# Gate and up projections as seven block products for eight, and a down projection over eight PSUM banks

## Chip, cores and metric

The kernel runs on one core of one Trainium2 chip. The metric is the device time of one launch in microseconds (us). All inputs start in HBM and the result ends there.

## What is computed

Two transformer blocks run one after the other on 512 tokens of width 1024, in float32. Each ends in a gated feed-forward network (FFN); the change touches these two FFNs and what stands next to them. Cut to that:

```python
# block 1, after attention
h = rms_norm(x, norm_ffn_pre)
f = (silu(h @ w_gate) * (h @ w_up)) @ w_down      # 1024 -> 2816 -> 1024
x = x + rms_norm(f, norm_ffn_post)
# block 2: mixer (pooling, stick-breaking attention, gates), then
h = rms_norm_2(x, norm_ffn)
x = x + (silu(h @ w_ffn_gate) * (h @ w_ffn_up)) @ w_ffn_down
gate = sigmoid(rms_norm_2(x, norm_ple) @ w_ple_gate)
x = x + gate * (p @ w_ple_proj)
return rms_norm_2(x, norm_final)
```

## The kernel before

**Precision.** A float32 matrix product is made from three products of a reduced format: each operand is split into a high part (a ScalarE copy) and a low part (a subtraction), and `mm3` (L138 to L140) adds hi·hi, hi·lo and lo·hi in one PSUM bank. So every weight tile of 128x1024 is loaded by a DMA on SP's queue (L131), its high part is made on ACT (L132) and its low part (L133) on DVE, or on POOL where `pl["lo"]` says so. Activations are split in the same way by `split_from` (L225, L226) and `split_many` (L213, L218).

**The FFN.** The 2816 hidden features are 22 f tiles of 128. For one f tile, `glu` multiplies the gate's and the up's weight tile (8 blocks of 128 input features each) with all 512 tokens: 2 x 8 x 3 = 48 matmuls of 128x512. Then come silu on ACT (L660), the product with up on DVE (L661, one operand in PSUM), and the split of the result, whose low part (L226) is POOL's. `ffn` takes the f tiles in three groups (6, 8, 8); after each group it loads that group's rows of the down weights and makes the down product, token tile by token tile (128 tokens, two banks of 512), and `evac` adds the banks to an SBUF accumulator (L707, L709, L1011).

**Where an FFN begins.** The first `NFIRST = 4` f tiles run on tokens 0 to 255 first and on tokens 256 to 511 afterwards, in matmuls of 256 columns, since the norms of token tiles 2 and 3 come late (`late_norm`, `norm_fill`; `tr_fill` transposes a normed tile with TensorE, L175, and splits it). The low parts of these tiles' weights are POOL's.

**Where an FFN ends.** The first FFN's last `evac1` calls `post_norm_then_pre` (L1073 to L1079): mean square on ACT (L166), reciprocal root on DVE (L148 to L159), scale by the gain row (L1076), add to x (L1077), norm again (`scale_rows`, L1070). x stays in SBUF, and is also written to memory (`spill` x2, L716) for block 2.

**What sets the order.** The program is written in Python loops over a tile framework, which gives each engine its own instruction order by priorities (`tc.high_priority`) and gives out buffers from pools. A new tile waits until the last reader of the buffer's old tile is done. All big loads are on SP's queue in one order, so a load that waits for its buffer holds back those behind it.

## Time and profile before

| | |
|---|---|
| time, median of 3 runs (lowest to highest) | 1372.39 us (1371.35 to 1376.75) |
| the profiled execution's own time, its span | 1375.31 us, 1373.5 us |
| TensorE clock granted, mean | 0.988 |
| busy: TensorE (PE), weight loads (PEld) | 1324.0 us (96%), 1080.8 us (79%) |
| busy: VectorE (DVE), ScalarE (ACT), GpSimd (POOL) | 715.1 (52%), 595.1 (43%), 250.2 (18%) |
| read from HBM | 130.14 MB, 101 GB/s over the span |

Times in the profile count from the span's start. The first FFN lies at about 231 to 612 us, the second at about 943 to 1308 us. Line numbers are those of the kernel before; where a line of the changed kernel is meant, the text says so.

### The profile page before, as it was taken

To read this page: it belongs to the slowest core of one execution; us is meant where nothing else is said; L and a number is where in the kernel's file an instruction comes from. 1 tells how busy PE (TensorE), PEld (TensorE's weight loads), DVE (VectorE), ACT (ScalarE), POOL (GpSimd) and SP (SyncE) were. 2 spreads that over 40 slices of the span, in tenths; PEclk is the share of its full clock that TensorE was granted. 3 is DMA by queue.
4 is the path that set the end of the run, shared out by engine and by line. 5 is a ranking of instruction groups with operands and counts; after the bars stand their busy time and mean duration, and the time that the engine had idled before them with its cause. 6 is when DMAs were issued, how large, how long until landed. Compare 5 with 4: busy or idle time off the path is not lost.

```text
span 1373.5 us, 17214 instructions
## 1 busy us (share of the span) xinstructions
PE 1324.0 (96%) x6476; PEld 1080.8 (79%) x6476; DVE 715.1 (52%) x1399; ACT 595.1 (43%) x1087; POOL 250.2 (18%) x255
## 2 busy tenths in 40 slices
PE   8889998899999999999999999989999999999997
PEld 6656666798888888878777778879988888888886
DVE  5889677742433242386886672655423321422464
ACT  5578876340322132244866564524413220422252
POOL 1433234320111011100323010115210110021002
PEclk9999999899999999999999999999999999999999
DMA  7212123241533143223121435634424330532031
GB/s 271 92 31 78 47 74 111 93 138 47 153 92 107 39 146 98 71 93 100 63 77 54 130 132 192 198 108 143 134 77 121 95 106 17 160 115 93 1 108 62
DMA packets 44771, 139.64 MB, mean 102 GB/s; under 512 B 7312, under 2 KB 7696, under 8 KB 44688
## 3 DMA queue, kind: packets, MB, share of 16 engines
q1 hardware_dynamic: 44544, 138.54, 31.8%
q8 instruction: 51, 0.84, 0.2%
q14 instruction: 32, 0.26, 0.1%
q10 hardware_dynamic: 144, 0.00, 0.0%
HBM read 130.14 MB, written 8.39 MB: 101 GB/s over the span
## 4 chain that ended last, share of the span: by engine, by line
PE 76%; DVE 9%; issue 7%; ACT 3%; POOL 2%; DMA 1%; POOLq 0%; ACTq 0%; DVEq 0%
PE acc L139 10%; PE acc L140 10%; PE acc L138 10%; PE f L140 10%; PE f L138 10%; PE f L139 10%; PE av L139 3%; PE av L138 3%; PE av L140 3%; DVE wt L133 2%; PE av L475 1%; DVE p L858 1%; PE tp L468 1%; DMA raw<-in_w_out 1%; PE tp L175 1%
## 5 line engine op out<-in xcount | busy, mean ns | idle before, releaser
L133 DVE TENSOR_TENSOR wt<-raw,wt 128x1024 fp32r<-128x1024 f32 (+1 forms) x204 | 254.2, 1247 | 280.8 <-ACT wt L132 279.8
L132 ACT ACTIVATE wt<-raw 128x1024 fp32r<-128x1024 f32 (+1 forms) x220 | 231.3, 1056 | 352.4 <-issue 84.2
L138 PE MATMUL f<-u,wt 128*128 128x512 f32 (+1 forms) x556 | 210.8, 379 | 4.3 <-DVE u L575 4.1
L139 PE MATMUL f<-u,wt 128*128 128x512 f32 (+1 forms) x556 | 210.0, 378 | 0.2 <-DVE u L218 0.2
L140 PE MATMUL f<-u,wt 128*128 128x512 f32 (+1 forms) x556 | 209.6, 377 | 0.0
L226 POOL TENSOR_TENSOR u<-t,u 128x512 fp32r<-128x512 f32 (+1 forms) x52 | 82.1, 1580 | 541.0 <-ACT u L225 541.0
L139 PE MATMUL acc<-u,wt 128*128 128x512 f32 (+1 forms) x432 | 155.0, 359 | 0.0
L138 PE MATMUL acc<-u,wt 128*128 128x512 f32 (+1 forms) x432 | 154.9, 359 | 0.0
L140 PE MATMUL acc<-u,wt 128*128 128x512 f32 (+1 forms) x432 | 154.8, 358 | 0.0
L138 PEld LDWEIGHTS f<-u,wt 128*128 128x128 f32 x556 | 106.3, 191 | 23.1 <-DVE u L575 4.3
L138 PE MATMUL f<-wt,u 128*128 128x512 f32 x302 | 120.6, 399 | 2.1 <-ACT u L225 2.1
L140 PE MATMUL f<-wt,u 128*128 128x512 f32 x302 | 119.9, 397 | 1.4 <-DVE u L226 1.4
L139 PEld LDWEIGHTS f<-u,wt 128*128 128x128 f32 x556 | 106.4, 191 | 17.1 <-DVE u L218 0.4
L140 PEld LDWEIGHTS f<-u,wt 128*128 128x128 f32 x556 | 106.4, 191 | 16.9
L139 PE MATMUL f<-wt,u 128*128 128x512 f32 x302 | 119.4, 396 | 0.0
L138 PE MATMUL acc<-wt,u 128*128 128x512 f32 (+1 forms) x288 | 112.7, 391 | 5.9 <-ACT wt L132 5.9
L139 PE MATMUL acc<-wt,u 128*128 128x512 f32 (+1 forms) x288 | 112.8, 392 | 1.6 <-DVE wt L133 1.5
L140 PE MATMUL acc<-wt,u 128*128 128x512 f32 (+1 forms) x288 | 112.4, 390 | 0.0
L138 PEld LDWEIGHTS acc<-u,wt 128*128 128x128 f32 x432 | 82.2, 190 | 12.0
L140 PEld LDWEIGHTS acc<-u,wt 128*128 128x128 f32 x432 | 82.0, 190 | 11.9
L139 PEld LDWEIGHTS acc<-u,wt 128*128 128x128 f32 x432 | 82.0, 190 | 11.8
L661 DVE TENSOR_TENSOR t<-t,acc 128x512 f32<-128x512 f32 (+1 forms) x52 | 31.4, 604 | 94.4 <-PE acc L140 91.3
(257 smaller groups left out, 2138.0 us busy)
## 6 DMA issues: line engine op xcount, KB each, us to landing
raw<-in_w_out SPq DMA_DIRECT2D x24, 512.0 KB, 3.7
raw<-in_w_gate SPq DMA_DIRECT2D x22, 512.0 KB, 3.6
raw<-in_w_up SPq DMA_DIRECT2D x22, 512.0 KB, 3.6
raw<-in_w_down SPq DMA_DIRECT2D x22, 512.0 KB, 3.6
raw<-in_w_ffn_gate SPq DMA_DIRECT2D x22, 512.0 KB, 3.5
raw<-in_w_ffn_up SPq DMA_DIRECT2D x22, 512.0 KB, 3.5
raw<-in_w_ffn_down SPq DMA_DIRECT2D x22, 512.0 KB, 3.5
raw<-in_w_in SPq DMA_DIRECT2D x11, 512.0 KB, 5.5
```

The source lines that it names most:

```text
L132: nc.scalar.activation(w[:, 0, c], raw[:, c], AF.Copy)
L133: pl["lo"].tensor_tensor(w[:, 1, c], raw[:, c], w[:, 0, c].bitcast(F32), op=ALU.subtract)
L138: nc.tensor.matmul(ps, lhsT=st[0], rhs=mv[0], start=first, stop=False)
L139: nc.tensor.matmul(ps, lhsT=st[0], rhs=mv[1], start=False, stop=False)
L140: nc.tensor.matmul(ps, lhsT=st[1], rhs=mv[0], start=False, stop=last)
L175: nc.tensor.transpose(pt[:, j * P:(j + 1) * P], h_t[:, k * P:(k + 1) * P], ident)
L226: (lo_eng or nc.vector).tensor_tensor(lo, src, hi.bitcast(F32), op=ALU.subtract)
L468: nc.tensor.transpose(pt[:, c:c + P], pn[j][:, kc * P:(kc + 1) * P], ident)
L475: nc.tensor.matmul(o[s * 64:s * 64 + 64], lhsT=VT[kc][:, kv], rhs=ts[s][:, i * 256:i * 256 + 256], start=kc == 0, stop=kc == NT - 1, skip_ ...
L661: nc.vector.tensor_tensor(s[:, :n], s[:, :n], pu[:, :n], op=ALU.mult)
L858: nc.vector.tensor_tensor_scan(c[:, n - 1::-1], ones.to_broadcast([P, n]) if nq == 1 else restart[:, :n], e[:, n - 1::-1], 0.0, op0=ALU.mu ...
```

## The change

Tokens are cut into two halves of 256 and the 1024 input features into two halves of 512; gate and up are the two block columns of one 2 by 2 block matrix. Seven products of blocks take the place of eight. Each product (`prod`, L309 of the changed kernel) has 4 feature blocks x 3 parts = 12 matmuls of 128x256, so an f tile has 84 of these.

- Left operands: a11 and a12 are transposed token rows as before (`left_raw`). a22 and four sums of blocks (p1, s2, s3, p4) come from `left_rest`: for each of two pairs of token tiles four subtractions of 128x512 on DVE, five blocks of four transposes, and their splits. An FFN has 56 transposes where it had 32.
- Right operands: `Tile.sums` forms four sums of weight halves on POOL (128x512, in place in the load buffers), one f tile ahead, and splits the two 1024-wide results; `prepare` loads both weight tiles and splits the gate's tile and half of the up's.
- `Tile.rest` combines the products: five DVE operations of 128x256 with one operand in PSUM, two silu of 128x256, one ACT copy, and one product of 128x512 on DVE. The low part of the result moves from POOL to DVE.
- The FFN begins with `NFIRST = 6` tiles, of which only the first two products run early; they need tokens 0 to 255 alone. Their gate weights' low parts are DVE's. Both late norms come before the FFN.
- f tiles come in groups (6, 5, 5, 6). `down` keeps all 4 x 2 PSUM banks open and goes through the group's f tiles with one 128x1024 row tile of the down weights at a time (528 matmuls of 128x512 for an FFN, as before), after the next group's first f tile. The last group goes token tile by token tile.
- x is written out before the first FFN and loaded again in `evac1`; the gain rows there use the load buffers (`raw_tile`, five in turn). The loads of the side input p move behind the second FFN.

```diff
-NFIRST = 4
+NFIRST = 6
...
+    GROUPS = (6, 5, 5, 6)
...
+    def raw_tile():
+        pools = pl["raws"]
+        cnt[4] += 1
+        return pools[cnt[4] % len(pools)].tile([P, 1024], F32, tag="raw", name=nm("raw"))
...
+    def left_rest(X, h0, h1, j):
+
+        c1, c2 = u_tile([P, 2, 512]), u_tile([P, 2, 512])
+        sub = nc.vector.tensor_tensor
+        sub(c1[:, 0], h1[:, 0:512], h1[:, 512:1024], op=ALU.subtract)
+        sub(c1[:, 1], h0[:, 0:512], c1[:, 0], op=ALU.subtract)
+        left_block(X, "s2", c1[:, 1], j)
...
+    def prod(ps, w, off, X, first):
+
+        for k in range(4):
+            x = X[k // 2][:, k % 2]
+            st = wcols(w, off + k * P, off + (k + 1) * P)
+            mv = (x[:, 0], x[:, 1])
+            for n, (a, b) in enumerate(((0, 0), (0, 1), (1, 0))):
+                nc.tensor.matmul(ps[:, :256], lhsT=st[a], rhs=mv[b], start=first and k == 0 and n == 0,
+                                 stop=k == 3 and n == 2, skip_group_check=True)
...
+        def prepare(self):
+
+            self.G, self.U = load_raw(self.wg[self.f]), load_raw(self.wu[self.f])
+            if not self.head:
+                self.wG = w8(self.G, pl["wt"])
+            self.w22 = w4(self.U[:, 512:1024])
+
+        def sums(self):
+
+            lo, hi = slice(0, 512), slice(512, 1024)
+            G, U = self.G, self.U
+            add = nc.gpsimd.tensor_tensor
+            add(G[:, lo], G[:, lo], U[:, lo], op=ALU.add)
+            add(U[:, lo], U[:, lo], U[:, hi], op=ALU.add)
+            add(U[:, hi], G[:, lo], U[:, hi], op=ALU.add)
+            self.wb = w8(U, wt1)
+            add(G[:, hi], U[:, hi], G[:, hi], op=ALU.add)
+            self.wa = w8(G, wt1)
...
+            if after:
+                after.first()
+            up = t_tile([P, 2, 256])
+            pn = any8()
+            prod(pn, wb, 512, X["s2"], True)
+            tt(E[:, 1], pn[:, h], E[:, 0], op=ALU.subtract)
+            pq = any8()
+            prod(pq, wb, 0, X["s3"], True)
+            tt(up[:, 1], E[:, 1], pq[:, h], op=ALU.subtract)
+            pr = any8()
+            prod(pr, wa, 0, X["p1"], True)
+            tt(up[:, 1], pr[:, h], up[:, 1], op=ALU.add)
+            if after:
+                after.second()
+            prod(pq, wa, 512, X["a22"], False)
+            tt(E[:, 3], pq[:, h], E[:, 1], op=ALU.subtract)
+            silu(E[:, 3], E[:, 3])
+            prod(pr, self.w22, 0, X["p4"], False)
+            tt(up[:, 0], pr[:, h], E[:, 1], op=ALU.add)
+            g = flat(up)
+            tt(g, E[:, 2:4].rearrange("p a b -> p (a b)"), g, op=ALU.mult)
...
+                g = T[f].rest(after if after and not after.head else None)
+                gT.append(u_tile([P, 2, S], F32R))
+                split_from(g, gT[-1][:, 0], gT[-1][:, 1])
+                if after:
+                    after.sums()
+                if held and f == f0:
+                    down(wdown, *held, acc, fresh)
+                    fresh, held = False, None
...
+    for tt in (2, 3):
+        with tc.high_priority(offset=PRIO_N):
+            norm_fill(tt)
+    for tt in range(NT):
+        nc.sync.dma_start(out=spill["x1"][tt], in_=x_t[tt])
+    block1.close()
+    ffn_phase()
...
+            rows[0] = [raw_tile() for _ in range(2)]
...
+        m, xt = acc1[tt], load_raw(spill["x1"][tt])
+        post_norm_then_pre(nc, m, xt, rows[0][0], rows[0][1], mean_square, rsqrt)
```

**DVE where the first FFN begins.** `u_511` is the normed row tile of token tile 3; its last norm operation is L1070 before and L1259 after. In the kernel before the rows around it are:

```order
L159 SCALAR_TENSOR_TENSOR rs_y1_712_2857<-rs_t1_713_2858,rs_y1_712_2857 128x1
L155 SCALAR_TENSOR_TENSOR rs_t1_713_2858<-rs_y1_712_2857,rs_a1_710_2855 128x1
L661 TENSOR_TENSOR t_716_2920<-t_716_2920,acc_715_2871 128x256
L159 SCALAR_TENSOR_TENSOR rs_y1_712_2857<-rs_t1_713_2858,rs_y1_712_2857 128x1
L661 TENSOR_TENSOR t_721_3001<-t_721_3001,acc_720_2952 128x256
L1070 SCALAR_TENSOR_TENSOR u_511_2159<-x_42_297,rs_y1_712_2857,row_565_2358 128x512 x2
L661 TENSOR_TENSOR t_724_3056<-t_724_3056,acc_723_3007 128x256
L661 TENSOR_TENSOR t_727_3111<-t_727_3111,acc_726_3062 128x256
L218 TENSOR_TENSOR u_617_2515<-tp_728_3116,u_617_2515 128x128
```

and in the changed kernel:

```order
L1259 SCALAR_TENSOR_TENSOR u_511_2159<-x_42_297,rs_y1_683_2776,row_565_2358 128x512 x2
L226 TENSOR_TENSOR wt_705_2830<-raw_704_2828,wt_705_2830 128x1024
L226 TENSOR_TENSOR wt_709_2863<-raw_708_2861,wt_709_2863 128x1024
L226 TENSOR_TENSOR wt_713_2896<-raw_712_2894,wt_713_2896 128x1024
L226 TENSOR_TENSOR wt_724_2980<-raw_723_2978,wt_724_2980 128x1024
L299 TENSOR_TENSOR u_715_2913<-u_501_2124 128x512
L302 TENSOR_TENSOR u_716_2914<-u_326_1483,u_501_2124 128x512
L300 TENSOR_TENSOR u_715_2913<-u_326_1483,u_715_2913 128x512
L306 TENSOR_TENSOR u_716_2914<-u_326_1483,u_715_2913 128x512
L226 TENSOR_TENSOR wt_728_3013<-raw_727_3011,wt_728_3013 128x1024
```

Before, the combining step of the first f tile (L661) stands among the norm's rows, and no weight split does, since the first tiles' are POOL's. After, the low parts of the first gate tiles (`wt_705` is that of f tile 0) stand behind the whole norm, with the four subtractions of `left_rest` behind them.

**DVE and POOL in the middle of an FFN.** One f tile of the kernel before has these rows on DVE (two weight tiles and the combining step):

```order
L661 TENSOR_TENSOR t_794_3754<-t_794_3754,acc_793_3705 128x512
L133 TENSOR_TENSOR wt_817_3955<-raw_816_3954,wt_817_3955 128x1024
L133 TENSOR_TENSOR wt_819_3960<-raw_818_3959,wt_819_3960 128x1024
L133 TENSOR_TENSOR wt_824_4020<-raw_823_4019,wt_824_4020 128x1024
L661 TENSOR_TENSOR t_801_3819<-t_801_3819,acc_800_3770 128x512
```

and one of the changed kernel:

```order
L372 TENSOR_TENSOR u_938_4926<-tp_958_5074,u_938_4926 128x256
L375 TENSOR_TENSOR t_957_5073<-u_938_4926,acc_959_5088 128x256
L226 TENSOR_TENSOR wt_962_5163<-raw_953_5051,wt_962_5163 128x1024
L378 TENSOR_TENSOR t_957_5073<-f_960_5102,t_957_5073 128x256
L226 TENSOR_TENSOR wt_963_5167<-raw_952_5049,wt_963_5167 128x1024
L226 TENSOR_TENSOR wt_980_5297<-raw_978_5293,wt_980_5297 128x1024
L382 TENSOR_TENSOR u_938_4926<-acc_959_5088,u_938_4926 128x256
L385 TENSOR_TENSOR t_957_5073<-f_960_5102,u_938_4926 128x256
L387 TENSOR_TENSOR t_957_5073<-u_938_4926,t_957_5073 128x512
L226 TENSOR_TENSOR u_961_5157<-t_957_5073,u_961_5157 128x512
L226 TENSOR_TENSOR u_968_5178<-raw_966_5173,u_968_5178 128x512
```

with these rows on POOL for one f tile, where before it had a single L226:

```order
L346 TENSOR_TENSOR raw_965_5171<-raw_965_5171,raw_966_5173 128x512
L347 TENSOR_TENSOR raw_966_5173<-raw_966_5173 128x512
L348 TENSOR_TENSOR raw_953_5051<-raw_952_5049,raw_953_5051 128x512
L350 TENSOR_TENSOR raw_952_5049<-raw_953_5051,raw_952_5049 128x512
L346 TENSOR_TENSOR raw_978_5293<-raw_978_5293,raw_979_5295 128x512
L347 TENSOR_TENSOR raw_979_5295<-raw_979_5295 128x512
L348 TENSOR_TENSOR raw_966_5173<-raw_965_5171,raw_966_5173 128x512
L350 TENSOR_TENSOR raw_965_5171<-raw_966_5173,raw_965_5171 128x512
```

DVE went from 3 rows for an f tile to 11, and POOL's from one that follows the combining step to four that precede the weight splits of a later f tile (`raw_965` and `raw_966` are a gate's and an up's load buffers).

**SP's queue where the first FFN ends.** Before:

```order
L131 DMA raw_1037_5525<-in_w_v 128x1024
L716 DMA spill_x2<-x_36_285 128x1024
L716 DMA spill_x2<-x_38_289 128x1024
L131 DMA raw_1039_5530<-in_w_v 128x1024
L716 DMA spill_x2<-x_40_293 128x1024
L131 DMA raw_1041_5535<-in_w_v 128x1024
L131 DMA raw_1051_5676<-in_w_q 128x1024
L131 DMA raw_1053_5681<-in_w_k 128x1024
L716 DMA spill_x2<-x_42_297 128x1024
```

and after:

```order
L249 DMA raw_1121_6403<-spill_x1 128x1024
L249 DMA raw_1104_6298<-spill_x1 128x1024
L898 DMA spill_x2<-raw_1089_6219 128x1024
L131 DMA raw_1168_6616<-in_w_v 128x1024
L898 DMA spill_x2<-raw_1104_6298 128x1024
L131 DMA raw_1170_6621<-in_w_v 128x1024
L898 DMA spill_x2<-raw_1121_6403 128x1024
L131 DMA raw_1172_6626<-in_w_v 128x1024
L131 DMA raw_1174_6631<-in_w_v 128x1024
L249 DMA raw_1138_6508<-spill_x1 128x1024
L898 DMA spill_x2<-raw_1138_6508 128x1024
L131 DMA raw_1184_6772<-in_w_q 128x1024
```

Before, the writes of x stand among the loads of the next weights. After, x is loaded as well, and the gain rows (L895, just ahead of these rows, `norm_ffn_post` first); x of token tile 3 (`raw_1138`) is one of the last, and the loads of `in_w_q` and all after it stand behind it.

## Rows read from the trace of the kernel before

**Rows 1.** The page, part 1: busy time of each engine, share of the span and instructions.

```profile
PE 1324.0 (96%) x6476; PEld 1080.8 (79%) x6476; DVE 715.1 (52%) x1399; ACT 595.1 (43%) x1087; POOL 250.2 (18%) x255
```

**Rows 2.** Stretches: busy us of each engine (instructions), granted TensorE clock, DMA share, GB/s.

```profile
230.00:265.00 35.00, 24.77 (x166) 23.99 (x165) 32.22 (x71) 13.88 (x27) 15.02 (x8) 0.80 0.34 106
255.00:260.00 5.00, 4.13 (x23) 4.16 (x24) 4.86 (x13) 1.60 (x5) 0.18 (x1) 0.59 0.71 228
...
290.00:570.00 280.00, 280.00 (x1256) 232.62 (x1255) 91.62 (x89) 77.13 (x93) 33.68 (x20) 1.00 0.32 100
...
940.00:1000.00 60.00, 60.00 (x455) 57.85 (x454) 27.51 (x53) 27.87 (x53) 22.42 (x14) 1.00 0.50 165
```

**Rows 3.** Timeline of PE, matmuls of 512 columns: start us, us, engine, line, operation, tiles.

```profile
506.73 0.39 PE L138 MATMUL acc<-u,wt 128*128 128x512 f32 x1
...
512.16 0.39 PE L138 MATMUL av<-u,wt 128*128 128x512 f32 x1
```

**Rows 4.** Timeline of PE, matmuls of 256 columns, and eight transposes of a token tile.

```profile
982.58 0.28 PE L138 MATMUL acc<-u,wt 128*128 128x256 f32 x1
...
985.46 0.28 PE L138 MATMUL av<-u,wt 128*128 128x256 f32 x1
...
270.02 1.04 PE L175 MATMUL tp<-ident,u 128*128 128x128 f32 x8
```

**Rows 5.** Timeline of DVE, end of the first pass over a tile's late tokens, both FFNs.

```profile
277.94 0.42 DVE L661 TENSOR_TENSOR t<-t,acc 128x256 f32<-128x256 f32 x1
...
974.14 0.42 DVE L661 TENSOR_TENSOR t<-t,acc 128x256 f32<-128x256 f32 x1 [0.23 <-PE acc L140]
```

**Rows 6.** Timeline of DVE: one token tile's norm at the first FFN's end.

```profile
579.61 0.15 DVE L148 TENSOR_SCALAR rs_a<-ms 128x1 f32<-128x1 f32 x1 [1.28 <-ACT t L166]
...
581.53 1.28 DVE L1076 SCALAR_TENSOR_TENSOR u<-u,rs_y,row 128x1024 f32<-128x1024 f32 x1
582.85 1.22 DVE L1077 TENSOR_TENSOR x<-x,u 128x1024 f32<-128x1024 f32 x1
...
587.26 1.42 DVE L1070 SCALAR_TENSOR_TENSOR u<-x,rs_y,row 128x512 f32<-128x512 f32 x2
```

**Rows 7.** Timeline of DVE, then POOL, in the stretch before the first FFN.

```profile
231.12 2.34 DVE L150 TENSOR_SCALAR rg<-rs_i 128x2 int32<-128x2 int32 x1
...
231.07 2.37 POOL L133 TENSOR_TENSOR wt<-raw,wt 128x1024 fp32r<-128x1024 f32 x1 [0.21 <-ACT wt L132]
```

**Rows 8.** Timeline of DVE and, below, POOL around one f tile of the first FFN.

```profile
305.72 0.69 DVE L661 TENSOR_TENSOR t<-t,acc 128x512 f32<-128x512 f32 x1 [2.65 <-PE acc L140]
306.79 1.23 DVE L133 TENSOR_TENSOR wt<-raw,wt 128x1024 fp32r<-128x1024 f32 x1 [0.39 <-ACT wt L132]
308.26 1.98 DVE L133 TENSOR_TENSOR wt<-raw,wt 128x1024 fp32r<-128x1024 f32 x1 [0.25 <-ACT wt L132]
...
307.36 1.81 POOL L226 TENSOR_TENSOR u<-t,u 128x512 fp32r<-128x512 f32 x1 [8.12 <-ACT u L225]
318.03 1.29 POOL L226 TENSOR_TENSOR u<-t,u 128x512 fp32r<-128x512 f32 x1 [8.86 <-ACT u L225]
```

**Rows 9.** Timeline of PE where the first FFN begins: in brackets the idle time before.

```profile
236.14 0.58 PE L138 MATMUL f<-u,wt 128*128 128x256 f32 x1 [4.05 <-DVE u L575]
```

**Rows 10.** Group of the page: ACT's high part of a 1024-wide weight tile (count, busy, mean ns).

```profile
L132 ACT ACTIVATE wt<-raw 128x1024 fp32r<-128x1024 f32 (+1 forms) x220 | 231.3, 1056 | 352.4 <-issue 84.2
```

**Rows 11.** Timeline of DVE and POOL at the second FFN's start; L218 has an operand in PSUM.

```profile
946.85 0.16 DVE L148 TENSOR_SCALAR rs_a<-ms 128x1 f32<-128x1 f32 x1 [2.52 <-ACT t L166]
...
947.19 0.29 DVE L218 TENSOR_TENSOR u<-tp,u 128x128 fp32r<-128x128 f32 x1
...
945.53 2.41 POOL L133 TENSOR_TENSOR wt<-raw,wt 128x1024 fp32r<-128x1024 f32 x1 [0.23 <-ACT wt L132]
```

**Rows 12.** The page, part 6: load of a gate weight tile, KB, us from issue to landing.

```profile
raw<-in_w_gate SPq DMA_DIRECT2D x22, 512.0 KB, 3.6
```

**Rows 13.** Timeline of PE behind the first FFN: the wait for its last norm.

```profile
615.47 0.65 PE L175 MATMUL tp<-ident,u 128*128 128x128 f32 x4 [1.35 <-DVE u L1070]
```

More of the change, by code (lines that the diff above doesn't have):

```diff
@@ new lines, in prod, with silu @@
+    def prod(ps, w, off, X, first):
+        for k in range(4):
+            x = X[k // 2][:, k % 2]
[4 more added lines that the diff above has]
+                                 stop=k == 3 and n == 2, skip_group_check=True)
+    def silu(out, src):
+        silus.append(nc.scalar.activation(out, src, AF.Silu))
@@ L720, in late_norm @@
-    def late_norm(tt):
-        with tc.high_priority(offset=PRIO_N):
-            norm_fill(tt)
-    ffn(hT, A["w_gate"], A["w_up"], A["w_down"], evac1,
-        {-1: [(late_norm, 2), (late_norm, 3)], (1, 0): [(tr_fill, 2)], (0, 256): [(tr_fill, 3)]})
+            nc.vector.tensor_tensor(acc1[tt][:, c], pss[cg], acc1[tt][:, c], op=ALU.add)
+        if tt == 0:
+            hT2[0] = new_hT()
+            rows[0] = [raw_tile() for _ in range(2)]
+            for t, nme in zip(rows[0], ("norm_ffn_post", "norm_mix_2")):
+                nc.sync.dma_start(out=t, in_=A[nme].partition_broadcast(P))
@@ L991, in transformer_pair, with evac2, rest2 @@
         scale_rows(nc, hn, xt, r, g_ffn)
-        flush()
-        pending.append((hn, hT, tt))
-        x_t.append(xt)
+        if tt in (1, 2):
+            raw2(tt - 1)
+        h_t.append(hn)
+        x_t.append(xt)
+    ffn_phase()
+    left_late(hX)
+    hT3 = [None]
+    def evac2(tt, pss):
+        xt = x_t[tt]
+        for cg in range(2):
+            c = slice(cg * 512, cg * 512 + 512)
+            nc.vector.tensor_tensor(xt[:, c], pss[cg], xt[:, c], op=ALU.add)
+        if tt == 0:
+            hT3[0] = new_hT()
+            rows[0] = raw_tile()
+            nc.sync.dma_start(out=rows[0], in_=A["norm_ple_2"].partition_broadcast(P))
+        r = rsqrt(mean_square(xt), 1)
+        hn = u_tile([P, D])
+        scale_rows(nc, hn, xt, r, rows[0])
+        flush()
+        pending.append((hn, hT3[0], tt))
+    def rest2(j):
+        left_rest(hX, h_t[j], h_t[2 + j], j)
+    ffn(hX, A["w_ffn_gate"], A["w_ffn_up"], A["w_ffn_down"], x_t, False,
+        {1: [(rest2, 0)], 3: [(rest2, 1)]}, evac2)
+    hT = hT3[0]
+    phase(wt=5, t=8, row=2, pT=2)
     pT = []
```

229 lines of the change are left out of this document (140 added, 89 removed).

## The prediction

> **What bounds the kernel now.** I read the page's busy shares first, then the stretches, then single timelines. TensorE works 96% of the span [rows 1]. Inside an FFN it has no gap at all: 280.00 us busy of 280.00, with DVE at 92 us, ACT at 77 and POOL at 34 [rows 2]. So there a saved matmul is saved time, and DVE, ACT and POOL have room, as long as none of them takes longer for an f tile than TensorE does. Where the first FFN begins the picture is another: 10.2 of 35 us idle, DVE busy for 32.2, and a granted clock of 0.59 in one stretch behind the idle time, so at the 1.2 GHz level for much of it [rows 2]. At the second FFN's start TensorE is full [rows 2].
>
> **What is removed.** A matmul of 512 columns follows the one before after 0.2267 us (24 of them from 506.73 to 512.16, 5.43 us [rows 3]), one of 256 columns after 0.120 (24 from 982.58 to 985.46, 2.88 us [rows 4]). An f tile was 48 x 0.2267 = 10.88 us, or 96 x 0.120 = 11.52 in the four head tiles; it becomes 84 x 0.120 = 10.08. That is 18 x 0.80 + 4 x 1.44 = 20.2 us for an FFN. The 24 added transposes cost 0.13 each (eight in 1.04 [rows 4]), 2.9 us or a little more. Net: **-17.3 us for an FFN, -34.6 in all**. The seven products save only 7% of the tile, not an eighth, since short matmuls are dearer by column. The down product keeps its 528 matmuls, 119.7 us.
>
> The Trainium skill ("TensorE: Matmul & The Clock Gate", section "Back-to-back issue gap") has a rule for the gap that gives 215.8 ns for 512 columns and 109.2 for 256. By it a tile would go from 10.36 to 9.17 us and the two FFNs would save about 18 us more (an estimate from that page). The rows measure 0.2267 and 0.120 in place of these, and the measurement decides.
>
> **The start of the first FFN.** Before, 277.94 is where the first tile's second pass has ended [rows 5]. Behind it lay 3 second passes (5.76 each), 18 tiles and the down product: 17.3 + 195.8 + 119.7 = 332.8, to 610.7. After, the corresponding point is the first `rest`. Behind it lie 22 x 10.08 less the two early products of six tiles (2.88 each), and the down product: 221.8 - 17.3 + 119.7 = 324.2. The question is when that `rest` begins.
>
> (a) DVE now runs both late norms ahead of the first gate tile's low part, which TensorE needs for its third matmul. One norm takes two reciprocal roots of 1.92 (579.61 to 581.53), 1.28, 1.22 and 1.42 [rows 6], so 7.8 us, two 15.5, and one to two waits of 1.28 for ACT's mean square. The head weights leave POOL, and with them go the 2.3 us that small DVE operations spent behind POOL's splits: one of 128x2 took 2.34 while POOL's ran from 231.07 for 2.37 [rows 7]; two of these lie right ahead of the norms. So DVE starts on the norms some 4 us before 238, at 234, ends them at 251 and the low part at 1.23 [rows 8] later: 252.4. Bounds 250.7 (no wait) and 256.5 (nothing gained from POOL). TensorE was idle from 232.1 (236.14 less 4.05 [rows 9]), so it now idles about 20 us for 10.2.
>
> (b) From 252.4 TensorE has 12 early products and 40 transposes, 17.3 + 5.2 us, and some 2 us of low clock (0.59 for 5 us [rows 2]): to 277. DVE has five gate splits (1.2), eight subtractions (0.65, from the 0.69 of 512 columns [rows 8]), 20 splits out of PSUM of 256 columns (0.42 [rows 5]), two of 512 and three of 1024: 6.0 + 5.2 + 8.4 + 1.3 + 3.6 = 24.5, to 276.9, and POOL's sums and ACT's high parts (1.06 [rows 10]) lie between these in a chain. I add 5 us of waits, between 0 and 10: **`rest` begins at 282**. Then 282 + 324.2 = 606.2 against 610.7: -4.5 where -17.3 was saved. So the start costs 12.8.
>
> **The start of the second FFN.** The last norm there has its first root at 946.85 [rows 11]; with 1.92 and 1.42 it ends at 950.2, and TensorE, which before had the split weights of four tiles for tokens 0 to 255, waits for the first gate tile's low part for about 6.6 us. The same 24.5 us of DVE work and 4 of waits give `rest` at 979: 979 + 324.2 = 1303.2 against 974.14 [rows 5] + 332.8 = 1306.9, so -3.7.
>
> **Tiles 1 to 5** run only their five late products, 7.2 us. The sums of tile f+1 stand on DVE and POOL behind the result of tile f: combine 0.42, two splits of 0.69, POOL's add 1.16, ACT 1.06, DVE 1.23, then the two products that they feed, 2.88: 8.1 us. Loss 1.1 x 4 tiles, 4.5 us for each FFN (0 if the order lets them overlap, 10 if every add waits for a DVE operation).
>
> **The other 16 tiles.** When POOL and DVE both read two SBUF operands, one waits for the other: DVE's split took 1.98 instead of 1.23, ending 1.07 after POOL's operation that ran into it (307.36 + 1.81); POOL's took 1.81 instead of 1.29, ending 1.15 after DVE's [rows 8]. With an operand in PSUM DVE is not held: 0.29 in the middle of POOL's 2.41 [rows 11]. An f tile has three splits of 1024, two of 512 and one product of 512 on DVE, and four adds on POOL. One after the other: 3 x 1.23 + 3 x 0.69 + 4 x 1.29 = 10.9 us at most; 3 x 1.07 + 3 x 0.53 + 4 x 1.15 = 9.4 at least (the 0.53 is 0.69 less the same 0.16). TensorE's 10.08 lies between. The other five DVE operations (0.42, PSUM) run beside POOL. I take 0.2 us of loss a tile, near the middle of the bounds, 3 us an FFN.
>
> The Trainium skill ("SBUF — State Buffer", section "Who interferes with whom") states this as a lock on a port pair for the whole of an instruction, when a DVE instruction has two SBUF inputs and GpSimd reads SBUF, and says that one SBUF input does not contend. By that rule the four adds speak against this change. The rows agree.
>
> **The end of the first FFN.** x of token tile 3 is now loaded, into the buffer that holds the gain row of norm_ffn_post, so its load (3.6 us [rows 12]) starts only after that row's last use, between two steps of the norm, and SP's later loads stand behind it. Before, TensorE waited 1.35 there [rows 13]; the last group's token tile is 8.2 us of matmuls instead of 10.9, against 7.8 of DVE's norm and its adds. I add 4.5 (0 to 8); 0.7 at the second end, where x stays.
>
> **The sum.** First FFN: -4.5 + 4.5 + 3 + 4.5 = +7.5. Second: -3.7 + 4.5 + 3 + 0.7 = +4.5. Together +12 on the profiled execution's 1375.3: 1387.3. That execution lies 2.9 above the median, so the forecast is **1384**. Loads and the memory are no term: DMA is a third busy [rows 2], and the 4 MB of x more are a few load times in all.
>
> **Rivals.** *Faster.* The adds fall into DVE's PSUM operations, `rest` begins at 277, and the end's load is hidden: what is left is the idle time of 10 and 6.6. 34.6 - 16.6 = 18 gained, 1354, or up to 1365 with half of the tile losses. For it: TensorE has no gap inside an FFN and DVE works a third of the time there [rows 2]. Against: 9.4 to 10.9 against 10.08.
>
> *Slower, the shared pair bounds.* If an f tile takes 10.7 to 11.3 (full durations, plus a wait per tile), 16 x 2 tiles lose 0.6 to 1.2 instead of 0.2: 13 to 33 more, 1397 to 1417. It decides from 10.08 up. For it: full durations are what most rows show. Against: DVE's five PSUM operations give POOL room.
>
> *The likeliest:* starts and end eat the saving, tiles nearly hold TensorE's pace, 1370 to 1397. This takes in a `rest` at 277 to 287.
>
> **Chances.** Faster rival 0.25, shared pair 0.20, the likeliest 0.55. About 0.5%, 6.9 us, can be told from no change: below 1365.5 is faster (0.27, the rival and the likeliest's low edge), above 1379.3 slower (0.52: the pair's 0.20, and three fifths of the likeliest), 0.21 between. With a tenth left out on either side the range is 1357 to 1408.
>
> **What would show it.** Right: matmuls of 256 columns at 0.120; idle time of about 20 us ahead of the first FFN's first products with DVE's norm named, and 6 at the second; POOL adds of 1.2 to 2.5 us; an f tile's pitch of 10.1 to 10.4; behind the last group a wait for x. Wrong: tiles at 10.08 without gaps and starts with less than 10 us idle (then it is faster), or a pitch over 10.7 with TensorE waiting for DVE's weight splits in each tile (then the pair).

## The result, and the profile after

The changed kernel takes **1451.14 us** (median of 4 runs, 1451.01 to 1452.35), against 1372.7 for the kernel before beside it: a ratio of 1.0568 [1.0545, 1.0591]. It is slower, as forecast, but by 78 us and not by 12, and lies 43 us above the range. The profiled span is 1449.4 us, 75.9 more than before.

The page, part 1, answers to [rows 1]:

```profile
PE 1324.3 (91%) x7724; PEld 1128.0 (78%) x7724; DVE 952.7 (66%) x1779; ACT 691.8 (48%) x1243; POOL 384.2 (27%) x363
```

TensorE is busy for as long as before, in a span that is 76 us longer, so it now stands idle for 125 us instead of 50. That the saved matmuls do not show in the busy time is in part the clock: its granted mean is 0.972 here and was 0.988, which makes some 81 us of the span at the 1.2 GHz level instead of 33 (an estimate from the two means). The stretches of [rows 2] in the same columns (the first begins at 228 here), and the second FFN's start:

```profile
228.00:265.00 37.00, 16.26 (x104) 14.38 (x103) 25.36 (x63) 13.60 (x23) 1.88 (x2) 0.72 0.31 111
290.00:570.00 280.00, 264.70 (x1798) 245.53 (x1797) 176.25 (x231) 108.11 (x154) 102.58 (x72) 0.99 0.30 97
980.00:1020.00 40.00, 29.30 (x202) 26.52 (x203) 26.58 (x46) 21.50 (x44) 11.58 (x8) 0.89 0.36 117
```

The middle of the first FFN, which had no gap at all, has 15.3 us of idle time in 280. No engine is full there: DVE is at 176 us and POOL at 103. So over the whole stretch no engine's work holds TensorE back; an order of steps may, or two engines that hold each other up.

**The short matmuls cost what was predicted.** In the timeline of PE 12 matmuls of 256 columns take from 432.13 to 433.57, 0.120 each, as in [rows 4]:

```profile
432.13 1.60 PE L316 MATMUL tp<-sh,wt 128*128 128x256 f32 x12
433.57 0.40 PE L316 MATMUL acc<-sh,wt 128*128 128x256 f32 x2
```

**The starts have nearly the size predicted.** The timeline of PE at the first FFN's start (against [rows 9]) and at the second's, with the first product and the first `rest` of each:

```profile
250.02 0.80 PE L316 MATMUL f<-u,wt 128*128 128x256 f32 x2 [19.59 <-ACT wt L225]
...
280.37 0.50 PE L316 MATMUL acc<-sh,wt 128*128 128x256 f32 x2 [0.84 <-ACT wt L225]
...
983.71 0.79 PE L316 MATMUL f<-u,wt 128*128 128x256 f32 x2 [6.51 <-ACT wt L225]
...
1016.15 0.51 PE L316 MATMUL tp<-sh,wt 128*128 128x256 f32 x2 [2.37 <-ACT wt L225]
```

Idle for 19.59 us where about 20 was forecast, and 6.51 where 6.6 was; `rest` begins at 280.37 (forecast: 282), and in the second FFN at 1016.15, 39.1 behind the block before (forecast: 35.6). Most of the loss came behind it: the last down product of the first FFN begins at 638.19 instead of 611.70, 26.5 later, where the terms gave 3.

**A wait inside the tiles.** The timeline of all engines around one f tile in the middle of the first FFN:

```profile
491.95 0.69 DVE L226 TENSOR_TENSOR u<-raw,u 128x512 fp32r<-128x512 f32 x1
...
492.72 1.29 POOL L346 TENSOR_TENSOR raw<-raw,raw 128x512 f32<-128x512 f32 x1 [7.28 <-DVE u L226]
...
494.09 1.30 POOL L347 TENSOR_TENSOR raw<-raw 128x512 f32<-128x512 f32 x1
...
495.35 1.29 POOL L348 TENSOR_TENSOR raw<-raw,raw 128x512 f32<-128x512 f32 x1
...
496.67 1.06 ACT L225 ACTIVATE wt<-raw 128x1024 fp32r<-128x1024 f32 x1 [4.57 <-POOL raw L348]
...
497.76 1.31 DVE L226 TENSOR_TENSOR wt<-raw,wt 128x1024 fp32r<-128x1024 f32 x1 [4.27 <-ACT wt L225]
...
499.00 0.41 DVE L378 TENSOR_TENSOR t<-f,t 128x256 f32<-128x256 f32 x1
...
499.46 2.93 PE L316 MATMUL f<-sh,u 128*128 128x256 f32 x12 [2.20 <-DVE t L378]
...
502.73 1.29 POOL L346 TENSOR_TENSOR raw<-raw,raw 128x512 f32<-128x512 f32 x1 [4.74 <-DMA raw<-in_w_up]
```

Here the adds take their undisturbed time, 1.29, but they start late and stand in a chain: DVE's split of `w22` must read the load buffer before the adds overwrite it, then come three adds in line, ACT's high part, and DVE's low part. DVE's PSUM operation L378, whose bank TensorE needs, stands behind the low part in DVE's order, and starts at 499.00 as that ends. TensorE then runs 12 matmuls in 2.73 us, at a granted clock of 0.50 (stretch 499.4 to 502.2), the 1.2 GHz level, behind an idle time of 2.20; that is 1.3 us more than at 0.120. The last row is the next tile's first add: it waits for a load that comes late. The waits of PE over the whole kernel (us in total, times, longest) count such gaps:

```profile
PE f L316 <- DVE t L378: 20.1, 12, 2.2
```

**Two engines that hold each other up.** The timeline of the same kernel near the FFN's beginning:

```profile
307.67 2.27 POOL L346 TENSOR_TENSOR raw<-raw,raw 128x512 f32<-128x512 f32 x1
...
308.85 1.46 PE L316 MATMUL acc<-sh,wt 128*128 128x256 f32 x10 [0.74 <-DVE wt L226]
309.05 1.97 DVE L226 TENSOR_TENSOR wt<-raw,wt 128x1024 fp32r<-128x1024 f32 x1
310.01 2.15 POOL L347 TENSOR_TENSOR raw<-raw 128x512 f32<-128x512 f32 x1
...
310.94 1.77 DVE L387 TENSOR_TENSOR t<-u,t 128x512 f32<-128x512 f32 x1
```

These adds of 1.29 take 2.27 and 2.15, the split of 1.23 takes 1.97, and a DVE product of 0.69 takes 1.77: each is held until the other engine's operation has ended, as in [rows 8].

### The profile page after: what moved, and what is told of

Same layout as the page of the kernel before. It is cut to its first block, busy times and chain, and to the rows that moved or that the text cites. A ratio compares the mean times of both kernels' runs of the same rounds, so it can differ in the third digit from the quotient of the medians.

```text
span 1449.4 us, 20541 instructions
## 1 busy us (share of the span) xinstructions
PE 1324.3 (91%) x7724; PEld 1128.0 (78%) x7724; DVE 952.7 (66%) x1779; ACT 691.8 (48%) x1243; POOL 384.2 (27%) x363
## 5 line engine op out<-in xcount | busy, mean ns | idle before, releaser
L226 DVE TENSOR_TENSOR wt<-raw,wt 128x1024 fp32r<-128x1024 f32 x176 | 231.8, 1327 | 179.2 <-ACT wt L225 178.7
L225 ACT ACTIVATE wt<-raw 128x1024 fp32r<-128x1024 f32 x176 | 184.8, 1057 | 263.7 <-POOL raw L348 130.6
L346 POOL TENSOR_TENSOR raw<-raw,raw 128x512 f32<-128x512 f32 x44 | 64.2, 1460 | 422.7 <-DVE wt L226 197.9
L133 DVE TENSOR_TENSOR wt<-raw,wt 128x1024 fp32r<-128x1024 f32 (+1 forms) x88 | 108.7, 1238 | 57.4 <-ACT wt L132 56.7
L316 PE MATMUL acc<-sh,wt 128*128 128x256 f32 x984 | 134.9, 285 | 4.3 <-DVE wt L226 1.8
L316 PEld LDWEIGHTS acc<-sh,wt 128*128 128x128 f32 x984 | 125.3, 193 | 6.5 <-DVE wt L226 2.7
L139 PE MATMUL f<-wt,u 128*128 128x512 f32 (+1 forms) x294 | 117.2, 399 | 5.0 <-DVE wt L133 2.8
L138 PE MATMUL f<-wt,u 128*128 128x512 f32 (+1 forms) x294 | 117.8, 402 | 1.8 <-ACT u L225 1.8
L140 PE MATMUL f<-wt,u 128*128 128x512 f32 (+1 forms) x294 | 117.6, 400 | 1.6 <-DVE u L226 1.6
L132 ACT ACTIVATE wt<-raw 128x1024 fp32r<-128x1024 f32 (+1 forms) x88 | 91.8, 1046 | 41.8 <-PE f L140 11.7
L138 PE MATMUL f<-u,wt 128*128 128x512 f32 x272 | 107.5, 395 | 0.3 <-ACT nx L937 0.2
L139 PE MATMUL f<-u,wt 128*128 128x512 f32 x272 | 107.1, 394 | 0.0
L140 PE MATMUL f<-u,wt 128*128 128x512 f32 x272 | 106.7, 392 | 0.0
L316 PE MATMUL tp<-sh,wt 128*128 128x256 f32 x552 | 77.1, 287 | 9.6 <-DVE wt L226 3.9
L348 POOL TENSOR_TENSOR raw<-raw,raw 128x512 f32<-128x512 f32 x44 | 60.5, 1376 | 93.5 <-DVE u L226 93.1
```

The costliest lines, as they stand in the source:

```text
L132: nc.scalar.activation(w[:, 0, c], raw[:, c], AF.Copy)
L133: pl["lo"].tensor_tensor(w[:, 1, c], raw[:, c], w[:, 0, c].bitcast(F32), op=ALU.subtract)
L138: nc.tensor.matmul(ps, lhsT=st[0], rhs=mv[0], start=first, stop=False)
L139: nc.tensor.matmul(ps, lhsT=st[0], rhs=mv[1], start=False, stop=False)
L140: nc.tensor.matmul(ps, lhsT=st[1], rhs=mv[0], start=False, stop=last)
L225: nc.scalar.activation(hi, src, AF.Copy)
```

## The experiments

Behind the result stood three theories, numbered as in the first four expectations. 1: latency, since the adds follow one another in a chain, and PSUM operations that TensorE needs stand behind weight splits in DVE's order. 2: GpSimd and DVE hold each other up. 3: loads come late, since the adds hold their load buffers. From experiment 5 on each expectation has theories of its own, under letters. The ratios are to the kernel before on the same chip; the changed kernel's 1451.1 is the reference for what an edit brings.

The experiments share one measure: the row of DVE's product of an f tile (L387 of the changed kernel), in the first, sixth and last tile of an FFN. Start us, then the two stretches: *head* (sixth less first) and *others* (last less sixth, with three down products). By matmuls alone *others* is 16 x 10.08, less one tile's two early products (2.88), plus 384 x 0.2267: 245.5; *head* is 4 x 7.2 + 10.08: 38.9, since its last tile also runs two early products of the next.

| kernel | first FFN: first tile | head | others | second FFN: first tile | head | others |
|---|---|---|---|---|---|---|
| changed kernel | 292.7 | 52.2 | 260.2 | 1028.2 | 53.7 | 262.1 |
| no adds | 287.7 | 39.2 | 245.6 | 990.8 | 40.4 | 245.9 |
| adds to scratch | 297.6 | 51.6 | 248.2 | 1021.1 | 51.6 | 248.1 |
| adds on DVE | 291.9 | 44.8 | 245.8 | 1003.0 | 44.6 | 246.6 |
| head's adds on DVE | 291.6 | 47.9 | 262.3 | 1024.6 | 46.6 | 261.0 |
| six load buffers | 294.8 | 50.5 | 253.4 | 1033.2 | 51.6 | 251.4 |

**1. No adds.** The kernel leaves the sums of weights out, so it computes another product.

```diff
-            add(G[:, lo], G[:, lo], U[:, lo], op=ALU.add)
-            add(U[:, lo], U[:, lo], U[:, hi], op=ALU.add)
-            add(U[:, hi], G[:, lo], U[:, hi], op=ALU.add)
             self.wb = w8(U, wt1)
-            add(G[:, hi], U[:, hi], G[:, hi], op=ALU.add)
```

> The changed kernel without its four GpSimd additions of weight halves per f tile: the two 1024-wide splits read the loaded weights themselves, so that the product is another one. Matmuls, DVE and ACT instructions are unchanged. The changed kernel takes 1451 us and loses some 65 us in the two stretches of f tiles. Theory 1 (latency: additions, ACT's high part and DVE's low part follow each other, and DVE's in-order queue holds the PSUM steps behind them): 45 to 60 us less, 1390 to 1406. Theory 2 (the pair shared by DVE and GpSimd): the same, 1390 to 1406. Theory 3 (five load buffers, loads come late): under 20 us less, above 1431.

Measured: 1385.02, ratio 1.008 [1.0051, 1.0109]; 66 of the 78 us are gone, and *others* is 245.6 where matmuls alone give 245.5. So with DVE's order as it was, TensorE is not held back in the tiles. The gain is more than the 45 to 60 that theories 1 and 2 gave, and does not tell them apart.

**2. The adds without anybody who needs them.** The same four adds write a scratch tile; the splits read the loaded weights.

```diff
+            s = pl["scr"].tile([P, 512], F32, tag="scr", name=nm("scr"))
-            add(G[:, lo], G[:, lo], U[:, lo], op=ALU.add)
+            add(s, G[:, lo], U[:, lo], op=ALU.add)
...
-            add(G[:, hi], U[:, hi], G[:, hi], op=ALU.add)
+            add(s, U[:, hi], G[:, hi], op=ALU.add)
...
```

> The changed kernel with its four GpSimd additions per f tile written to a scratch tile that nobody reads, and the splits reading the loaded weights themselves (another product is computed): GpSimd reads and works as much as before beside DVE, but nothing waits for it except the buffers. Theory 1 (latency of the chain): 35 to 60 us less than 1451, that is 1391 to 1416. Theory 2 (shared pair): within 10 us of 1451. Theory 3 (load buffers): above 1431.

Measured: 1427.72, 1.0391 [1.0361, 1.0421], between the theories' ranges, and the table says why. The head is as slow as with the real adds (51.6), so there the mere presence of the adds beside DVE is enough; the other tiles lose 2.6 and 2.2 us instead of 14.6 and 16.2, so there it is that somebody waits for the adds. The timeline of DVE in this kernel's head over about one tile:

```profile
302.36 1.97 DVE L226 TENSOR_TENSOR wt<-raw,wt 128x1024 fp32r<-128x1024 f32 x1
304.25 0.41 DVE L383 TENSOR_TENSOR u<-tp,u 128x256 f32<-128x256 f32 x1
304.58 1.98 DVE L226 TENSOR_TENSOR wt<-raw,wt 128x1024 fp32r<-128x1024 f32 x1
306.48 0.41 DVE L386 TENSOR_TENSOR t<-acc,u 128x256 f32<-128x256 f32 x1
307.00 1.26 DVE L388 TENSOR_TENSOR t<-u,t 128x512 f32<-128x512 f32 x1
308.18 0.41 DVE L373 TENSOR_TENSOR u<-f,u 128x256 f32<-128x256 f32 x1
308.95 0.99 DVE L226 TENSOR_TENSOR u<-t,u 128x512 fp32r<-128x512 f32 x1 [0.36 <-ACT u L225]
309.86 1.75 DVE L226 TENSOR_TENSOR u<-raw,u 128x512 fp32r<-128x512 f32 x1
311.53 0.41 DVE L376 TENSOR_TENSOR t<-u,av 128x256 f32<-128x256 f32 x1
```

The five operations with both operands in SBUF take 7.95 us; undisturbed they are 2 x 1.23 + 3 x 0.69 = 4.53. The four on PSUM keep 0.41. DVE comes to the same split again after 9.5 us (302.36 to 311.86), where TensorE has 7.2 of work in a head tile.

**3. DVE's order.** The low parts of the two sums are queued behind the PSUM operations L378 and L382.

```diff
             self.wb = w8(U, wt1)
+            if prev:
+                queue_after(last_split[0], prev.c378)
...
             self.wa = w8(G, wt1)
+            if prev:
+                queue_after(last_split[0], prev.c382)
```

> The changed kernel with DVE's order alone changed: the low part of one tile's first sum comes behind the third PSUM step of the tile before (L378 of the changed kernel), that of the second sum behind the fourth (L382). All else is the same. Theory 1 with the order as its main part: 10 to 25 us less than 1451, 1426 to 1441, and TensorE's waits for L378 (20.1 us) gone. Theory 2 and theory 3: within 4 us of 1451.

Measured: 1461.03, 1.0633 [1.0603, 1.0664], 10 slower than the change, which no theory had. *Others* grows to 266.7 and 266.4. TensorE's waits for that third PSUM operation fall from 22.6 us to 2.9, as expected, but its waits for ACT's copy of the next tile's first product rise from 4.1 to 22.1. So the order is not the cause by itself: these waits go when it is changed, and others take their place. How later low parts lead to the waits for ACT stays open.

**4. One load buffer more** (and one buffer less for the tiles' results, to make room).

```diff
-        phase(sh=10, raw2=3, wt=2, t=4)
-        pl["raws"] = [rawp] * 2 + [pl["raw2"]] * 3
+        phase(sh=10, raw2=4, wt=2, t=3)
+        pl["raws"] = [rawp] * 2 + [pl["raw2"]] * 4
```

> The changed kernel with six load buffers in turn in the FFNs instead of five (and three buffers instead of four for the combining tiles, to make room). Theory 3 (loads come late, since a buffer is held until its sum is split): 15 to 40 us less than 1451, 1411 to 1436. Theories 1 and 2: within 5 us of 1451.

Measured: 1439.19, 1.0474 [1.0444, 1.0505], 12 less. *Others* gains 7 and 11 us; from the first FFN's last tile to the second's first it loses 11. There TensorE waits 3.85 and 6.39 us behind the first FFN, for the norm and for the next weights, where it waited 2.21 and 2.76 in the changed kernel; whether that comes of the turn of the load buffers, which x and the gain rows take too, or of the buffer less for results, no run shows. The adds hold their load buffers until the splits have read the sums, and SP's next loads go into these. The waits of SP's queue in the changed kernel, 290 to 570:

```profile
SPq L249 <- DVE wt L226: 251.4, 43, 14.5
```

With a sixth buffer this wait is as long (251.6). The row tells who frees the buffers, and not that loads are late: in these 280 us SP's queue waits for some buffer for 261 us in the kernel before, 263 in the changed one and 271 without adds. That a load can be late shows in the add at 502.73 above. Of the 14.6 and 16.2 us that *others* loses against the kernel without adds, the buffer gives back 6.8 and 10.7. The gain in all, 12 us, lies between what theory 3 had (15 to 40) and what the others had (within 5).

**5. The adds on DVE.**

```diff
-            add = nc.gpsimd.tensor_tensor
+            add = nc.vector.tensor_tensor
```

> The changed kernel with the four additions of weight halves per f tile on DVE instead of GpSimd; all else is the same. The run without additions took 1385 us, the one with additions that nobody waits for 1428. Theory A (GpSimd is the cost: the shared pair in the head tiles, the slow chain of 1.3 us additions in the others): 45 to 60 us less than 1451, 1391 to 1406, since an addition of 512 from SBUF takes DVE 0.69 us and DVE's work for a tile, 7.1 plus 2.4 us, stays under TensorE's 10.08. Theory B (DVE's load for a tile is what bounds, wherever the additions run): not under 1430.

Measured: 1401.78, 1.0209 [1.0189, 1.023], 49 less, by giving more work to the busier engine. The timeline of DVE in the middle of the first FFN shows the adds:

```profile
489.38 0.69 DVE L348 TENSOR_TENSOR raw<-raw,raw 128x512 f32<-128x512 f32 x1
489.98 0.68 DVE L347 TENSOR_TENSOR raw<-raw 128x512 f32<-128x512 f32 x1
490.58 0.41 DVE L378 TENSOR_TENSOR t<-f,t 128x256 f32<-128x256 f32 x1
490.92 0.68 DVE L350 TENSOR_TENSOR raw<-raw,raw 128x512 f32<-128x512 f32 x1
491.52 1.22 DVE L226 TENSOR_TENSOR wt<-raw,wt 128x1024 fp32r<-128x1024 f32 x1
```

An add follows the one before after 0.60 us here, 1.26 to 1.37 on GpSimd, and nothing on DVE is stretched: L387 takes 678 to 1812 ns in the changed kernel and 679 to 693 in this one. The four adds are 2.4 us of DVE a tile, and the window 290 to 570 has TensorE at 277.72 of 280. Theory A of this expectation holds. The head stays at 44.8 against 39.2 without adds; I put that down to DVE's own added work in tiles of 7.2 us, which no run takes apart.

**6. The ends.** Gain rows and x go into free buffers of the left operands (`sh`), and the side input p is loaded inside the last group.

```diff
-            rows[0] = [raw_tile() for _ in range(2)]
+            rows[0] = [pl["sh"].tile([P, 1024], F32, tag="sh", name=nm("she")) for _ in range(2)]
...
-        m, xt = acc1[tt], load_raw(spill["x1"][tt])
+        m, xt = acc1[tt], pl["sh"].tile([P, 1024], F32, tag="sh", name=nm("she"))
+        nc.sync.dma_start(out=xt, in_=spill["x1"][tt])
...
```

> The changed kernel with the ends changed alone: gain rows and x are loaded into the buffers of the left operands (free once the last products are done) instead of the five load buffers, and the side input p is loaded and split during the second FFN's last group, not behind it. The changed kernel loses 8 us more than the kernel before between the FFNs and 7 us behind the second. Theory A (these loads and the queue behind them): 10 to 15 us less than 1451, 1436 to 1441. Rival (the last group's token tile of 8.2 us is too short for the norm's chain on DVE, whatever is loaded when): the wait for p goes (5 to 7 us), the rest stays, 1444 to 1446.

Measured: 1441.29, 1.0497 [1.0476, 1.0518], 10 less, at the edge of what theory A had. But not all of it lies at the ends. Of the 11.9 us by which the span is shorter, 2.1 lie between the first FFN's last product row and the second's first, and 3.0 behind the second's last; 8.3 lie in *others* (258.1 and 255.9), for which no cause was found. So some 5 of the 14.9 us that the two ends had cost (below) are shown to go, and at the first end TensorE still waits for DVE's low parts (below).

**7. The start.** The first four head tiles' gate weights go to the pool `wt1`, whose memory is free early.

```diff
-                self.wG = w8(load_raw(wg[f]), pl["wt"])
+                self.wG = w8(load_raw(wg[f]), wt1 if f < 4 else pl["wt"])
```

> The changed kernel with the first four gate tiles' splits in the pool wt1, which outlives the phases, instead of the new phase's pool wt, whose memory the first FFN gets only when the block's rows are done with (ACT's first high part waits for the last norm, L1259, at 248.9 us). Theory A (the wait for that memory is what keeps TensorE idle for 19.6 us): the first products start some 15 us earlier, and 8 to 18 us of the time go, 1433 to 1443. Theory B (DVE's work ahead of the first complete tile bounds, and it only changes places): 0 to 4 us, above 1447.

Measured: 1436.06, 1.0459 [1.0436, 1.0479], 15 less. The 19.59 us are gone from the first product, which follows the block before at about 231, so buffers held it. The second FFN gains as well: its first product waits 2.96 us instead of 6.51. Two waits for the late norms come in their place, in the timeline of PE:

```profile
248.00 1.94 PE L286 MATMUL tp<-ident,u 128*128 128x128 f32 x8 [3.80 <-DVE rs_y L159]
...
254.63 1.95 PE L286 MATMUL tp<-ident,u 128*128 128x128 f32 x8 [3.15 <-DVE rs_t L155]
```

**8. Edits 5, 6 and 7 together** (diffs as above).

> The changed kernel with the additions on DVE, the ends from the left operands' buffers and the head weights in wt1 together. If the three gains add up as theory A has them: 1451 - 50 - 12 - 12 = 1377, between 1362 and 1395. If the starts and ends are bound by DVE: 1395 to 1410.

Measured: 1379.91, 1.0042 [1.0028, 1.0057]. The three alone gave 49, 10 and 15; together they give 71, so they hardly overlap. With these three eased, the change is still 6 us slower than the kernel before.

**9. Seven products only behind the head.** Three head tiles go back to eight products in two halves of the tokens, as before, and seven products start with tile 4; the rest is as in 8.

```diff
-NFIRST = 6
+NFIRST = 3
...
+        for half in range(2):
+            aa = ("a11", "a12") if half == 0 else ("a21", "a22")
+            for f in range(NFIRST):
+                for w in hw[f]:
+                    pp.append(any8())
+                    prod(pp[-1], w, 0, X[aa[0]], True)
+                    prod(pp[-1], w, 512, X[aa[1]], False)
...
```

> A version from what the runs showed: additions on DVE, ends from the left operands' buffers, and the FFN's first three f tiles in the manner of the kernel before (all eight block products, tokens 0 to 255 first, then 256 to 511), so that the sums of blocks are made under 17 us more of matmuls; the seven products begin with the fourth tile. The first two head tiles' weights are in wt1. For an FFN 19 tiles at 10.08 and 3 at 11.52 us stand against 18 at 10.88 and 4 at 11.52 (15.8 less), with 32 more transposes (4.2 more): 23 us less in both than the kernel before. If the starts are as in the kernel before and the ends as in the run with all three changes (5 to 9 us worse than before): 1356 to 1363. If DVE's work ahead of the seven products still holds TensorE at the starts (10 us): 1366 to 1376.

Measured: 1372.25, 0.9991 [0.998, 1.0001]: 8 less than in 8, level with the kernel before, in the second of the two ranges.

**10. The writes of x on ACT's DMA queue** (on top of 9), so that no load stands behind them.

```diff
-        nc.sync.dma_start(out=spill["x2"][tt], in_=xt)
+        nc.scalar.dma_start(out=spill["x2"][tt], in_=xt)
```

> The same version with the four writes of x at the first FFN's end issued from ACT's queue instead of SP's, where the loads of the next weights (in_w_v) stand behind them. Theory A (those loads come late because of the writes): 3 to 5 us less than the version with the writes on SP. Rival (the loads wait for their buffers or ACT, or ACT is held by the write): within 1.5 us of it, or slower.

Measured: 1371.59, 0.9988 [0.9979, 0.9997]. That is within 1.5 us of experiment 9, so the theory of 3 to 5 us there falls: the writes ahead of those loads cost nobody that much.

**11. Only the head's adds on DVE** (the changed kernel otherwise).

```diff
-            add = nc.gpsimd.tensor_tensor
+            add = nc.vector.tensor_tensor if self.head else nc.gpsimd.tensor_tensor
```

> The changed kernel with the additions of the six head tiles alone on DVE, those of the other 16 tiles on GpSimd as they are. By the pitches of the f tiles, the run without additions gained some 33 us in the two heads and 29 in the other tiles. Theory A (both places pay): about half of what the move of all additions gave (49 us), 1422 to 1431. Rival 1 (the head is all): 1402 to 1410. Rival 2 (the other tiles are all): above 1443.

Measured: 1436.03, 1.0458 [1.0436, 1.0479]: 15 of the 49 us, less than the half expected. The heads gain 4.3 and 7.1, *others* nothing (+2.1 and -1.1). The four head tiles that run only late products fall from 10.0 and 10.4 us to 8.5 and 8.2, but the fifth, beside which GpSimd's adds for the later tiles already run, rises from 12.1 to 13.8. The larger part of the 49 lies in the other tiles.

**12. Buffers laid out so that the second FFN's first weights need no late memory** (on top of 10).

```diff
-            X[n] = [pl["sh"].tile([P, 2, 2, 256], F32R, tag="sh", name=nm("sh")) for _ in range(2)]
+            p = "sha" if n in ("a22", "p1") else "sh"
+            X[n] = [pl[p].tile([P, 2, 2, 256], F32R, tag="sh", name=nm("sh")) for _ in range(2)]
...
-        phase(sh=10, raw2=3, wt=2, t=4)
+        phase(wt=2, t=4, sha=4, raw2=3, sh=6)
+        cnt[4] = -1
...
-    phase(wt=5, t=8, row=2)
+    phase(wt=6, t=8, row=2)
```

> The version of the last call with the memory of the starts laid out anew and nothing else: the FFN phase's weight pool lies over buffers that the attention has done with, not over the rows of the norm, so the third head tile's weights need not wait for it; the second FFN's first tile finds two weight buffers and two load buffers free beside the product before it (one more buffer in that phase). The version before waits for ACT's high parts and DVE's norm for 12.4 us at the first start and 5.9 us at the second. Theory A (buffers hold the weights back): 5 to 10 us less than its 1371.6, 1361 to 1367, and clear of the kernel before. Theory B (at the first start DVE's norms and splits bound, only the second start pays): 2 to 5 us less, 1367 to 1370. Theory C (TensorE waits for the transposes of late norms in any order): within 1.5 us.

Measured: **1364.97, 0.9931 [0.9918, 0.9945]**, faster than both kernels, though by only 0.7% than the kernel before, and in theory A's range. The second FFN's start waits 1.38 and 0.76 us instead of 2.63 and 2.91, and its last f tile's product comes 3.5 earlier; the other 2.8 of the 6.3 us of span lie behind that FFN, and no single cause of them was found. The stretches, in the columns of [rows 2]:

```profile
228.00:265.00 37.00, 27.51 (x200) 25.89 (x199) 28.64 (x78) 14.05 (x27) 0.00 (x0) 0.86 0.33 117
290.00:570.00 280.00, 278.42 (x1949) 261.55 (x1948) 207.53 (x311) 115.95 (x168) 1.95 (x3) 1.00 0.35 114
```

The longest wait of PE that is left is at the first FFN's start, for the late left operands:

```profile
PE tp L322 <- DVE sh L218: 8.3, 1, 8.3
```

## Why the prediction was wrong

Against its own terms the 75.9 us divide up so (the prediction's sum was 12):

| term | predicted | measured |
|---|---|---|
| matmuls, both FFNs | -34.6 | -34.6 (0.120 a matmul) |
| start of the first FFN, to `rest` | +12.8 | +11.2 |
| start of the second FFN | +13.6 | +17.1 (`rest` 39.1 behind the block before, not 35.6) |
| left over behind `rest`, each FFN | 0 | +5.0, +5.1 |
| tiles 1 to 5 | +4.5, twice | +13.0, +13.3 |
| the other 16 tiles | +3, twice | +14.6, +16.2 |
| behind the first FFN | +4.5 | +7.0 (block 2's transposes come 33.5 later, the FFN's end 26.5) |
| behind the second FFN | +0.7 | +7.9 |

The losses of tiles are the table's columns less those without adds. In the first FFN -17.3 + 11.2 + 13.0 + 14.6 gives 21.5 of the 26.5 by which its end is late, so 5.0 are left over. In the second the block before ends 33.6 later and the last product 68.0 later, so the FFN itself takes 34.4 more, of which 5.1 are left in the same way. The prediction had all transposes ahead of `rest`; the trace has some among its first matmuls (at 280.72 and 282.65). What is left over is not the adds': by the same sum it is 5.3 and 9.5 in the kernel without adds, whose `rest` begins earlier, at 275.42 and 974.62. Up to the first product row the adds cost 5.0 us in the first FFN (292.7 and 287.7), and these lie ahead of `rest`, inside the term of the start.

**The direction was right, and the starts were nearly.** A saving of 17.3 us an FFN is mostly eaten by a start that must wait for the norms of all tokens. But the cause that "The start of the first FFN" gave for the first product was wrong: DVE ends the last norm at 248.9, and ACT makes the first gate tile's high part only then. The timeline of ACT:

```profile
248.91 2.00 ACT L225 ACTIVATE wt<-raw 128x1024 fp32r<-128x1024 f32 x2 [3.39 <-DVE u L1259]
```

ACT waited for an operation that it doesn't read: the norm was the last reader of rows and x, whose memory the FFN's new pool `wt` takes. Experiment 7 took that away and the product came 19 us earlier. The forecast of this wait was right by luck: both chains end with the same norm.

**The step that failed first is "Tiles 1 to 5".** It took the time of a head tile from a chain with undisturbed durations, 8.1 us, and so a loss of 1.1 (its own terms give 0.9, so 3.7 us an FFN and not 4.5). The step behind it had worked out what an f tile takes when DVE and GpSimd hold each other up, 9.4 to 10.9 us, and compared that with TensorE's 10.08; but a head tile has 7.2 us of TensorE's work. With two splits of 1024 instead of three the same sum is 2 x 1.23 + 3 x 0.69 + 4 x 1.29 = 9.7. Measured were 10.0 and 10.4 us on average over the four tiles with 7.2 us of work, 10.8 and 10.7 with adds that nobody waits for, and 7.4 and 7.7 without adds; the loss over tiles 1 to 5, 13.0 and 13.3, lies above the step's own bound of 10. The mechanism stood in the text, for the wrong tiles. It need not be all: from 300 to 340 DVE is busy for 31.1 of 40 us in the changed kernel, and for 36.7 with scratch adds, so with the real adds DVE also waits.

**The second is "The other 16 tiles".** 0.2 us a tile for the shared pair was right for what it named: adds to scratch cost 2.6 and 2.2 us in 16 tiles. What it left out is that the adds are a chain. Four adds in place, behind a split that must read the buffer first and ahead of two splits, hold load buffers until the last split; a load can come late, the next add with it (4.74 us at 502.73), and 12 times in the kernel TensorE waits for L378, some 1.7 us on average, and can pay again at the low clock behind it (1.3 us at 499.46). Moving the adds to DVE removes 14.4 and 15.5 us there. How much of that is the buffers' and how much the line of adds is open: a sixth buffer gave 7 and 11. Adds into buffers of their own were not tried. In the head, how far the chain adds to the lock is open too, since scratch adds run at other moments than the real ones.

The Trainium skill ("SBUF — State Buffer", section "Who interferes with whom") names the lock of the two engines; the trace agrees with it in the operations above (1.23 to 1.97, and 0.41 unmoved with an operand in PSUM).

**The ends were undersized.** "The end of the first FFN" named a load that does come late: x of the last token tile is loaded at 645.32 and DVE waits for it, and the next weights' low part waits behind that. The timelines of SP, DVE and PE:

```profile
645.32 0.33 SPq L249 DMA_DIRECT2D raw<-spill_x  x1
...
649.84 1.22 DVE L1266 TENSOR_TENSOR raw<-raw,u 128x1024 f32<-128x1024 f32 x1 [0.56 <-DMA raw<-spill_x]
650.98 1.22 DVE L133 TENSOR_TENSOR wt<-raw,wt 128x1024 fp32r<-128x1024 f32 x1
...
652.25 0.50 PE L139 MATMUL f<-wt,u 128*128 128x512 f32 x1 [2.76 <-DVE wt L133]
```

This is the place of [rows 13], 7 us instead of 4.5. But the load is not the cause by itself: in experiment 6 DVE no longer waits for x, and TensorE still waits 2.41 and 3.32 us there for low parts of the next weights, which stand behind the norm's steps in DVE's order. That speaks for the rival of that expectation, the norm's chain on DVE beside token tiles of 8.2 us. At the second end 0.7 had no term for the loads of p, which the change moves there; the timeline of PE shows what they cost, 3.62 us and then matmuls at 0.43 instead of 0.2267:

```profile
1381.26 0.79 PE L138 MATMUL av<-wt,pT 128*128 128x512 f32 x1 [3.62 <-ACT pT L225]
1381.86 0.63 PE L139 MATMUL av<-wt,pT 128*128 128x512 f32 x1
1382.28 0.63 PE L138 MATMUL acc<-wt,pT 128*128 128x512 f32 x1
```

**The range was too narrow** since the rival "the shared pair bounds" multiplied its loss by 16 tiles and left the head at 8.1. The other tiles did come at that rival's time, 11.0 and 11.1 us each once the down products are taken off, but not for its reason: with scratch adds they take 10.25. No rival let the adds be late; "What would show it" named a sign close to what came, TensorE waiting for DVE's weight splits, where it waits for the PSUM operation behind such a split. One estimate is off without effect: the 18 us more that two FFNs would save by the formula for the gap set a saving before the transposes against one behind them; like with like it is 13.
